# A two-layer streaming encoder on one core: half of layer 0's second shift is read later, three up groups are computed without it, and its output projection is split except for two units

## The chip, the core and the metric

The kernel runs on one core of a Trainium2 chip, one launch for the whole function. The metric is device time in microseconds (us). Arrays are float32.

## What is computed

Two layers over 256 positions of 2048 channels, with one conditioning vector c. What matters of a layer (LN is a layer norm, ALPHA a constant; the four mixers between are not touched by the change):

```
mod = silu(c) @ w_mod[l] + b_mod[l]            # 2048 -> 6 x 2048
shift_m, scale_m, gate_m, shift_f, scale_f, gate_f = mod
h = LN(x) * (1 + scale_m) + shift_m
y = concat(mixers(h @ w_in[l])) @ w_out[l]     # output projection, 2048 x 2048
x = LN(ALPHA * x + (1 + gate_m) * y)
h = LN(x) * (1 + scale_f) + shift_f
gate, val = split(h @ w_up[l])                 # 2048 -> 2 x 5632
y = (silu(causal_conv3(gate) + b_conv) * val) @ w_down[l]
x = LN(ALPHA * x + (1 + gate_f) * y)
```

shift_f is a vector over channels, the same for every position; so its part of `h @ w_up` is one number per column of w_up: `shift_f @ w_up`.

## The kernel before

**Products.** A weight of 1 MB is loaded as `wraw` (two k-tiles of 128 rows by 1024 columns, or four of 512). ScalarE (ACT) casts each half to fp32r as `whi` (L344), VectorE (DVE) writes the rest as `wlo` (L345); activations are split in the same way by `split` (L361: `a`, `hT`). A split product on TensorE (PE) is hi x hi + hi x lo + lo x hi. A plain product takes the fp32 weight `wexact` (0.5 MB a load) and the unsplit activations in one matmul instruction; each of those has two records in the trace. `weights` (L314) makes either kind.

**The output projection.** `out_proj` (L574) makes the 2048 output columns in the chunks 1024, 512 and 512 (`CHUNKS`, L572), each over all 16 k-tiles in units. For layer 0 the second and third chunk, and the first two units of the first (`PLAIN_UNITS`), are plain (`exact`, L703); layer 1 splits all of it. `finish` (L601) applies gate and residual, `norm` (L632) the layer norm, and `to_hN` (L549) turns the result (`ps_xT`, PE) and applies scale and shift into `hN`: four pieces per quarter and half of the positions, on ACT or DVE. k-tile kt of `h` is channels 128 kt to 128 kt + 127.

**The FFN's up projection.** `ffn_up` (L1373) goes through groups of 512 columns: first gate group 0 (`first_group`, L490, plain, straight from `hN`), whose result is turned and copied into `g` (L1405); then value group v0, gate group g1, v1, g2, v2 and so on (`group2`, L417), each four units of four k-tiles, from `hT`, the split of `hN` (L364, L363). Each gate block's convolution and SiLU, `gate_conv` (ACT at L120 and L1418, DVE at L1415), waits in the list `background` and is taken two at a unit; `valued` (L1420) multiplies a value group in.

**The modulation.** Each 128 columns of w_mod are one step of `mods` (L255): a load of 1 MB `wmod`, issued by the SP queue (L192), and one DVE instruction that multiplies by the replicated silu(c) and sums (L193), 192 steps in all. They are a generator, in the fixed order of L255: a layer's shift, scale and gate vectors of 16 steps each. At each unit, `pump` adds the rate of the phase (`RATES`, L35) and takes as many steps as are due; `need` takes those that are missing before a vector is used. A gate vector is turned into a row, written to DRAM (`line`) and read back to all partitions (`gate`) by `gate_rows` (L231). `wmod`, `wraw` and `wlate` tiles share one pool of raw buffers.

The program's order on each engine is the order in which this code calls it, except where a unit's products are held back one step (`pending`, `postponed`).

Of the kernel before, what the change touches and what calls it, by code (L numbers as in the profile page):

```python
# [35 lines left out]
    dict(B=1.3, attend=1.3, C=1.9, out=1.0, out_next=1.55, out_last=0.0, up=0.7, down=0.7, down_next=0.7, down_last=0.0),  # L36
    dict(D=1.0, U=0.0, V=0.0, B=0.0, C=0.0, E=0.9, attend=0.0, out=0.6, out_next=0.6, out_last=0.0, up=0.3, down=0.7, down_next=0.7, down_last=0.0),
# [7 lines left out]
PLAIN_UNITS = 2  # L45

# [40 lines left out]
def encoder_kernel(ctx: ExitStack, tc: tile.TileContext, A: dict, consts: bass.AP, out: bass.AP):  # L87
# [122 lines left out]
    def mod_stream(order):  # L210
        for l, m in order:
            yield from column_steps(l, m)
        while chores:
            yield
            chore()

    def column_steps(l, m):
        sums = keep.tile([P, KT], F32, name=f"sums_{l}_{m}")
        for kt in range(KT):
            last_step[0] = mod_block(l, m, kt, sums[:, kt : kt + 1]).ins.name  # L220
            if kt == KT - 1:
                cols = keep.tile([P, KT], F32, name=f"mod_{l}_{m}")
                dve.tensor_tensor(out=cols, in0=sums, in1=bcol[l][:, m * KT : (m + 1) * KT], op=ALU.add)
                for j in range(KT):
                    MOD[(l, m, j)] = cols[:, j : j + 1]
                if m in (GATE_M, GATE_F):
                    chores.extend(gate_rows(l, m, cols))
            yield
            chore()

    def gate_rows(l, m, cols):  # L231
# [3 lines left out]
        def turn():  # L235
            if pace["phase"] == "up":
# [19 lines left out]
        [(0, GATE_M), (0, SHIFT_F), (0, SCALE_F), (0, GATE_F), (1, SHIFT_M), (1, SCALE_M)]  # L256
# [14 lines left out]
    def need(l, m):  # L271
        rows = m in (GATE_M, GATE_F)
        while (l, m) not in GATE if rows else (l, m, KT - 1) not in MOD:
# [275 lines left out]
    def to_hN(t, q, r, l, m_shift, m_scale, after=None):  # L549
# [10 lines left out]
        for j in range(4):  # L560
            src, dst = ps[:, j * P : (j + 1) * P], hN[q][:, j, t * P : (t + 1) * P]
            sc, sh = MOD[(l, m_scale, 4 * q + j)], MOD[(l, m_shift, 4 * q + j)]
            if t == 0 or j % 2 == 0:
                last_norm[1] = ident_act(dst, src, sc, sh)
                turned[q] = last_norm[1].ins.name
            else:
# [7 lines left out]
    def out_proj(l, stage, w, src, order, gate_of, name, post_g, post_b, before, then, plain=(), bg=0):  # L574
# [112 lines left out]
        for c0, width in CHUNKS:  # L687
# [11 lines left out]
            def load_unit(u, c0, width, nk, units, last):  # L699
# [3 lines left out]
                exact = c0 in plain or (bool(plain) and u < PLAIN_UNITS)  # L703
# [669 lines left out]
    def ffn_up(l, G):  # L1373
# [3 lines left out]
        for c0 in range(0, D_FF, 512):  # L1377
            gi, j0 = c0 // 512, c0 // P

# [10 lines left out]
            def gated(cps, j0=j0):  # L1390
# [3 lines left out]
                for i in range(4):  # L1394
                    background.append(lambda j=j0 + i: gate_conv(j))

            def gated_first(t, ps):
# [8 lines left out]
                if t == 1:  # L1406
                    for i in range(4):
                        background.append(lambda j=i: gate_conv(j))
# [10 lines left out]

            def valued(cps, j0=j0):  # L1420
# [8 lines left out]
            else:  # L1429
                run(group2(w, c0, f"g{l}{gi}", gated))  # L1430
            run(group2(w, D_FF + c0, f"v{l}{gi}", valued, bg=STEPS[l]["up"]))
# [93 lines left out]
    for l in range(DEPTH):  # L1525
# [5 lines left out]
        else:  # L1531
# [14 lines left out]
            plain=(1024, 1536) if l == 0 else (),  # L1546
            bg=STEPS[l]["out"],
        )
        phase(l, "up")
# [47 lines left out]

def _constants():
# [25 lines left out]
def build(inputs):  # L1624
# [7 lines left out]
    direct.update(params=_params(v), gmlp=_gmlp(v), consts=_constants())  # L1632
# [21 lines left out]
```

## Time and profile before

| | |
|---|---|
| median of 3 runs | 2214.95 us (2213.76 to 2219.54) |
| the profiled execution | 2214.94 us |
| its span on the core | 2213.2 us |
| PE busy | 2185.3 us (99%) |
| DVE busy | 1702.1 us (77%) |
| ACT busy | 1075.7 us (49%) |
| POOL (GpSimd) busy | 22.4 us (1%) |
| read from HBM | 604.17 MB, 274 GB/s over the span |

Busy time is a mean over stages. PE is busy nearly always, so the kernel's time is PE's work plus PE's waits; where PE waits, the row of PE's timeline has the wait in square brackets, with what ended it. A matmul's row is longer than the step from one product to the next, since products overlap in the array: a rate is read from the starts of two rows, not from a row's length.

### The profile page before, as it was taken

Reading aid. Unit: us, or ns where it says so; the run is one execution under the profiler, and the core shown is the slowest. Engines: PE = TensorE matmul, PEld = TensorE weight load, DVE = VectorE, ACT = ScalarE, POOL = GpSimd, SP = SyncE. Lnnn points to the kernel's source line nnn. Section 1 sums busy time; section 2 is a strip of 40 time slices with the busy share of each in tenths; the row PEclk is TensorE's granted clock in tenths of the full one; section 3 lists DMA queues with packets and bytes.
Section 4 is the critical chain, followed back from the end, with each engine's and each line's share of the span. In section 5 each row is a group of like instructions: output and inputs, shape, how many; then the busy total and the mean of one; then the engine's idle time right before and its main releaser. Section 6 shows DMA issues by size and latency. Waiting matters only on the chain. (4 is left out here: it accounts for less than half of the span.)

```text
span 2213.2 us, 28318 instructions
## 1 busy us (share of the span) xinstructions
PE 2185.3 (99%) x10852; PEld 1794.0 (81%) x10852; DVE 1702.1 (77%) x2265; ACT 1075.7 (49%) x1652; POOL 22.4 (1%) x38
## 2 busy tenths in 40 slices
PE   9999999999999999999999999999999999999997
PEld 6776875588888888888867988868888888888886
DVE  5657996799898888989958988877765656565776
ACT  3132730655454545545665455465444545464553
POOL 0000000000000000000000000000000000000000
PEclk9999999999999999999999999999999999999999
DMA  9999889598888888888757547856765555555553
GB/s 391 417 376 391 358 332 390 210 350 324 310 333 318 327 313 324 344 332 326 285 215 294 189 157 255 316 210 246 265 211 190 190 190 191 190 210 192 191 195 145
DMA packets 94730, 608.15 MB, mean 275 GB/s; under 512 B 10689, under 2 KB 10881, under 8 KB 29313
## 3 DMA queue, kind: packets, MB, share of 16 engines
q1 hardware_dynamic: 94466, 606.31, 74.0%
q8 instruction: 85, 1.39, 0.2%
q14 instruction: 51, 0.42, 0.0%
q10 hardware_dynamic: 128, 0.03, 0.0%
HBM read 604.17 MB, written 2.13 MB: 274 GB/s over the span
## 5 line engine op out<-in xcount | busy, mean ns | idle before, releaser
L345 DVE TENSOR_TENSOR wlo<-wraw,whi 128x1024 fp32r<-128x1024 f32 (+1 forms) x608 | 729.0, 1214 | 286.3 <-ACT whi L344 273.1
L344 ACT CAST whi<-wraw 128x1024 fp32r<-128x1024 f32 (+1 forms) x608 | 630.9, 1045 | 635.4 <-PE g_c L117 207.8
L193 DVE SCALAR_TENSOR_TENSOR wmod<-wmod,crep 128x2048 f32<-128x2048 f32 x192 | 438.4, 2287 | 72.0 <-DMA wmod<-in_w_mod_dram 71.1
L117 PE MATMUL v_c<-hT,whi 128*128 128x512 f32 x1408 | 489.7, 393 | 0.0
L117 PE MATMUL g_c<-hT,whi 128*128 128x512 f32 x1280 | 445.0, 392 | 0.0
L117 PE MATMUL v_c<-hT,wlo 128*128 128x256 f32 x1408 | 392.5, 279 | 0.0
L117 PE MATMUL d<-whi,a 128*128 128x512 f32 x1344 | 386.5, 389 | 0.0
L117 PE MATMUL g_c<-hT,wlo 128*128 128x256 f32 x1280 | 356.8, 279 | 0.4 <-DVE wlo L345 0.4
L117 PEld LDWEIGHTS v_c<-hT,whi 128*128 128x128 f32 x1408 | 263.6, 187 | 59.2
L117 PEld LDWEIGHTS d<-whi,a 128*128 128x128 f32 x1344 | 252.0, 188 | 52.4
L117 PEld LDWEIGHTS g_c<-hT,whi 128*128 128x128 f32 x1280 | 239.7, 187 | 54.1
L117 PEld LDWEIGHTS v_c<-hT,wlo 128*128 128x128 f32 x1408 | 265.4, 188 | 0.2
L117 PEld LDWEIGHTS g_c<-hT,wlo 128*128 128x128 f32 x1280 | 241.2, 188 | 0.7 <-DVE wlo L345 0.7
L117 PE MATMUL d<-wlo,a 128*128 128x512 f32 x672 | 232.9, 389 | 0.0
L117 PEld LDWEIGHTS d<-wlo,a 128*128 128x128 f32 x672 | 126.1, 188 | 26.2
L363 ACT CAST a<-g 128x512 fp32r<-128x512 f32 x132 | 81.3, 617 | 63.8 <-PE d L117 63.2
L364 DVE TENSOR_TENSOR a<-g,a 128x512 fp32r<-128x512 f32 x132 | 89.0, 686 | 5.1 <-ACT a L363 5.1
L117 PE MATMUL o<-whi,a 128*128 128x512 f32 x320 | 91.6, 393 | 0.0
L501 PE MATMUL first<-wexact,hN 128*128 128x512 f32 x192 | 85.5, 595 | 1.4 <-ACT hN L120 1.0
L1415 DVE SCALAR_TENSOR_TENSOR u<-g,par,u 128x254 f32<-128x254 f32 (+1 forms) x176 | 73.8, 477 | 0.0
L117 PEld LDWEIGHTS o<-whi,a 128*128 128x128 f32 x320 | 60.6, 190 | 12.7
L501 PEld LDWEIGHTS first<-wexact,hN 128*128 128x128 f32 x192 | 35.3, 190 | 41.2 <-issue 34.9
(311 smaller groups left out, 2174.0 us busy)
## 6 DMA issues: line engine op xcount, KB each, us to landing
wmod<-in_w_mod_dram SPq DMA_DIRECT2D x192, 1024.0 KB, 7.2
wraw<-in_ffn_w_up_dram SPq DMA_DIRECT2D x168, 1024.0 KB, 5.1
wraw<-in_ffn_w_down_dram SPq DMA_DIRECT2D x88, 1024.0 KB, 5.0
wexact<-in_w_in_dram SPq DMA_DIRECT2D x64, 512.0 KB, 11.0
wraw<-in_w_in_dram SPq DMA_DIRECT2D x24, 1024.0 KB, 6.1
wraw<-in_w_out_dram SPq DMA_DIRECT2D x22, 1024.0 KB, 6.0
wexact<-in_w_out_dram SPq DMA_DIRECT2D x20, 512.0 KB, 11.6
wexact<-in_ffn_w_up_dram SPq DMA_DIRECT2D x16, 512.0 KB, 5.7
```

The costliest lines, as they stand in the source:

```text
L117: pe.matmul(o, lhsT, rhs, start=start, stop=stop, skip_group_check=True)
L193: i = dve.scalar_tensor_tensor(out=raw, in0=raw, scalar=1.0, in1=crep, op0=ALU.mult, op1=ALU.mult, accum_out=col)
L344: held(act.copy(hi[:, :m], r), "cast")
L345: i = dve.tensor_tensor(out=lo[:, :m], in0=r, in1=hi[:, :m].bitcast(F32), op=ALU.subtract)
L363: act.copy(hi, src)
L364: dve.tensor_tensor(out=lo, in0=src, in1=hi.bitcast(F32), op=ALU.subtract)
L501: i = pe.matmul(ps, hN[kt // 4][:, kt % 4, t * P : (t + 1) * P], parts[kt], start=kt == 0, stop=kt == KT - 1, skip_group_check=True,)
L1415: dve.scalar_tensor_tensor(out=u[:, sh:], in0=x[:, : S - sh], scalar=col(k, j), in1=u[:, sh:], op0=ALU.mult, op1=ALU.add)
```

## The change

- The second and third chunk of layer 0's output projection are made of split products, as in layer 1; the first two units of the first chunk stay plain. With 512 columns a chunk has 8 units.
- The order of the modulation steps is now: gate_m, scale_f, the first 8 k-tiles of shift_f, its last 8 (the late half), 4 steps of gate_f, six new steps (`late_steps`), the rest of gate_f, and so on. `need` asks only for the first 8 k-tiles of layer 0's shift_f. The rate is 0 in chunks two and three, 1.0 in the first gate group and v0 (phase `up_first`), and 0.75 after.
- `to_hN` leaves the shift out for k-tiles 8 to 15 of layer 0's FFN (12 pieces on ACT, 4 on DVE, with one operand less). Gate groups 0 and 1 and value group 0 are computed with that input, three groups of 512 columns.
- In g1, as soon as a unit's products are issued, `renewing` rewrites the hT of that unit's k-tiles, if they are among 8 to 15, with the shift: 8 ACT and 8 DVE instructions of 128x256. v1 and all later groups use it.
- The late half of the vector is made a row (`late_row`: a write to DRAM and a read of 0.5 MB to all partitions, both issued by GpSimd), and `late_steps` load the 1536 columns of w_up for the three groups transposed (six loads of 1 MB, `late`, laid out on the host) and sum them with the row on DVE: 12 instructions of 128x1024, one number per channel.
- That number is added to a gate block ahead of its convolution (`gate_late`, 8 on ACT) and to a value block where it is multiplied in (`value_late`, 4 on DVE and 2 products). Until then v0 and v1 are kept in `value` tiles.

The numbers of instructions go on PE from 10014 to 10142, on DVE from 2051 to 2089, on ACT from 1598 to 1632, on the SP queue from 659 to 657 and on POOL from 43 to 45.

```diff
-    dict(B=1.3, attend=1.3, C=1.9, out=1.0, out_next=1.55, out_last=0.0, up=0.7, down=0.7, down_next=0.7, down_last=0.0),
+    dict(B=1.3, attend=1.3, C=1.9, out=1.0, out_next=0.0, out_last=0.0, up_first=1.0, up=0.75, down=0.7, down_next=0.7, down_last=0.0),
...
+LATE = 8
...
+    def column_steps(l, m, k0=0, k1=KT):
...
+                if (l, m) == (0, SHIFT_F) and k1 == KT:
+                    chores.append(lambda: late_row(cols[:, LATE:KT]))
...
+    def late_row(cols):
+        line = dramp.tile([P, KT - LATE], F32, name="line_late")
+        pool.dma_start(out=line, in_=cols)
+        late["row"] = gatep.tile([P, D], F32, tag="gate", name="late_row")[:, : (KT - LATE) * P]
+        pool.dma_start(out=late["row"], in_=line.rearrange("p k -> (p k)").partition_broadcast(P))
+        return True
+
+    def late_steps():
+        n = (KT - LATE) * P
+        for i in range(6):
+            raw = raw_tile("wlate")
+            nc.sync.dma_start(out=raw, in_=A["late"][i])
+            for h in range(2):
+                part = raw[:, h * n : (h + 1) * n]
+                dve.scalar_tensor_tensor(
+                    out=part, in0=part, scalar=1.0, in1=late["row"], op0=ALU.mult, op1=ALU.mult,
+                    accum_out=late["sums"][:, 2 * i + h : 2 * i + h + 1],
+                )
+            if i % 2 == 1:
+                background.extend(late["then"].pop(0))
+            yield
+            chore()
...
-        [(0, GATE_M), (0, SHIFT_F), (0, SCALE_F), (0, GATE_F), (1, SHIFT_M), (1, SCALE_M)]
+        [(0, GATE_M), (0, SCALE_F), (0, SHIFT_F, 0, LATE), (0, SHIFT_F, LATE, KT)]
+        + [(0, GATE_F, 0, 4), late_steps, (0, GATE_F, 4, KT), (1, SHIFT_M), (1, SCALE_M)]
...
+        last = LATE - 1 if (l, m) == (0, SHIFT_F) else KT - 1
...
+            without = (l, m_shift) == (0, SHIFT_F) and 4 * q + j >= LATE
...
-                exact = c0 in plain or (bool(plain) and u < PLAIN_UNITS)
+                exact = u < plain and c0 == 0
...
+                if l == 0 and j0 < 8:
+                    late["then"].append([lambda j=j0 + i: gate_late(j) for i in range(4)])
...
+            def gate_late(j):
+                x = G[j // 4][:, j % 4, :]
+                ident_act(x, x, 1.0, late["sums"][:, j : j + 1])
+                gate_conv(j)
...
+            def value_late(i):
+                v0, v1 = late["values"]
+                for j in (2 * i, 2 * i + 1):
+                    g = G[0][:, j, :]
+                    dve.scalar_tensor_tensor(
+                        out=g, in0=v0[:, j, :], scalar=late["sums"][:, 8 + j : 9 + j], in1=g, op0=ALU.add, op1=ALU.mult
+                    )
+                g = G[1][:, 2 * i : 2 * i + 2, :]
+                dve.tensor_tensor(out=g, in0=g, in1=v1[:, 2 * i : 2 * i + 2, :], op=ALU.mult)
...
+    def renewing(g):
+        units, load, products, end, bg = g
+        def then(item, u):
+            products(item, u)
+            for kt in range(max(LATE, 4 * u), 4 * u + 4):
+                h, col = hN[kt // 4][:, kt % 4, :], MOD[(0, SHIFT_F, kt)]
+                hi, lo = (x[:, kt % 2, :] for x in hT[kt // 2][:2])
+                ident_act(hi, h, 1.0, col)
+                dve.scalar_tensor_tensor(
+                    out=lo, in0=h, scalar=col, in1=hi.bitcast(F32), op0=ALU.add, op1=ALU.subtract
+                )
+        return units, load, then, end, bg
...
-            plain=(1024, 1536) if l == 0 else (),
+            plain=PLAIN_UNITS if l == 0 else 0,
```

**VectorE where v0 starts.** The last splits of `hT`, the modulation steps, the two copies of gate group 0's result and the first weights of v0 (`wlo`), before:

```order
L364 TENSOR_TENSOR hT_2332<-hN3_2169,hT_2332 128x2x256
L193 SCALAR_TENSOR_TENSOR wmod_2368,sums_0_5_2367<-wmod_2368,crep_104 128x2048
L364 TENSOR_TENSOR hT_2333<-hN3_2169,hT_2333 128x2x256
L193 SCALAR_TENSOR_TENSOR wmod_2371,sums_0_5_2367<-wmod_2371,crep_104 128x2048
L345 TENSOR_TENSOR wlo_2377<-wraw_2374,whi_2376 128x1024
L345 TENSOR_TENSOR wlo_2381<-wraw_2374,whi_2380 128x1024
L193 SCALAR_TENSOR_TENSOR wmod_2384,sums_0_5_2367<-wmod_2384,crep_104 128x2048
L1405 COPY g_2350<-ps_gT_2353 128x4x128
L1405 COPY g_2350<-ps_gT_2361 128x4x128
```

and with the change:

```order
L402 TENSOR_TENSOR hT_2494<-hN3_2331,hT_2494 128x2x256
L402 TENSOR_TENSOR hT_2495<-hN3_2331,hT_2495 128x2x256
L195 SCALAR_TENSOR_TENSOR wmod_2529,sums_0_3_1599<-wmod_2529,crep_104 128x2048
L195 SCALAR_TENSOR_TENSOR wmod_2532,sums_0_3_1599<-wmod_2532,crep_104 128x2048
L195 SCALAR_TENSOR_TENSOR wmod_2535,sums_0_3_1599<-wmod_2535,crep_104 128x2048
L195 SCALAR_TENSOR_TENSOR wmod_2538,sums_0_3_1599<-wmod_2538,crep_104 128x2048
L1461 COPY g_2512<-ps_gT_2515 128x4x128
L1461 COPY g_2512<-ps_gT_2523 128x4x128
L383 TENSOR_TENSOR wlo_2544<-wraw_2541,whi_2543 128x1024
```

Four steps in a row and the copies now stand ahead of v0's first `wlo`; before, two steps did, and both `wlo` came ahead of the copies.

**ScalarE in g1.** The casts of g1's third unit (`whi_2807`, `whi_2811`), the rewriting of k-tiles 8 to 11 (`hT_2492`, `hT_2493`) and the casts of the fourth unit, with the change:

```order
L382 CAST whi_2807<-wraw_2805 128x1024
L382 CAST whi_2811<-wraw_2805 128x1024
L122 ACTIVATE hT_2492<-hN2_2330,mod_0_3_1600 128x256 x2
L122 ACTIVATE hT_2493<-hN2_2330,mod_0_3_1600 128x256
L382 CAST whi_2853<-wraw_2851 128x1024
L382 CAST whi_2857<-wraw_2851 128x1024
L122 ACTIVATE hT_2493<-hN2_2330,mod_0_3_1600 128x256
```

Three of the four new instructions stand ahead of the fourth unit's casts; before, nothing stood between the casts of two units there.

**VectorE in g2.** The end of the late sums, the work with them, and the weights of g2's last unit (`wlo_3314`), with the change:

```order
L383 TENSOR_TENSOR wlo_3262<-wraw_3259,whi_3261 128x1024
L383 TENSOR_TENSOR wlo_3266<-wraw_3259,whi_3265 128x1024
L258 SCALAR_TENSOR_TENSOR wlate_3301,late_118<-wlate_3301,late_row_2693 128x1024 x2
L1479 SCALAR_TENSOR_TENSOR g_2512<-value_2742,late_118,g_2512 128x256 x2
L1483 TENSOR_TENSOR g_2951<-g_2951,value_3170 128x512
L1479 SCALAR_TENSOR_TENSOR g_2512<-value_2742,late_118,g_2512 128x256 x2
L1483 TENSOR_TENSOR g_2951<-g_2951,value_3170 128x512
L383 TENSOR_TENSOR wlo_3314<-wraw_3311,whi_3313 128x1024
```

All the rows between the two units' `wlo` are new at this place.

## Rows read from the trace of the kernel before

**Rows 1.** The page: span, and busy time of each engine with its instructions.

```profile
span 2213.2 us, 28318 instructions
PE 2185.3 (99%) x10852; PEld 1794.0 (81%) x10852; DVE 1702.1 (77%) x2265; ACT 1075.7 (49%) x1652; POOL 22.4 (1%) x38
```

**Rows 2.** The chain that ended last: start us, us, what. Layer 1, split groups.

```profile
1518.14 22.19 PE g_c L117 x128
...
1961.98 239.42 PE d L117 x1056
```

**Rows 3.** Stretch of chunks two and three: us, busy of PE, PEld, DVE, ACT, POOL; PEclk, DMA.

```profile
346.16:401.10 54.94, 54.94 (x130) 24.27 (x129) 33.87 (x57) 7.34 (x18) 1.55 (x2) 1.00 0.95 382
```

**Rows 4.** VectorE's timeline: start us, us, line, operation; layer 0, ahead of chunk two.

```profile
341.45 2.28 DVE L193 SCALAR_TENSOR_TENSOR wmod<-wmod,crep 128x2048 f32<-128x2048 f32 x1
...
343.87 1.29 DVE L604 TENSOR_TENSOR yg<-o,gate 128x512 f32<-128x512 f32 x2
```

**Rows 5.** TensorE's timeline where the projection ends: layer 0, then layer 1.

```profile
401.10 1.04 PE L557 MATMUL ps_xT<-cst,xn 128*128 128x128 f32 x8
402.24 3.70 PE L501 MATMUL first<-wexact,hN 128*128 128x512 f32 x8
...
1462.26 0.39 PE L117 MATMUL o<-whi,a 128*128 128x512 f32 x1
...
1464.09 0.70 PE L501 MATMUL first<-wexact,hN 128*128 128x512 f32 x1
```

**Rows 6.** VectorE's timeline where v0 starts.

```profile
425.00 0.68 DVE L364 TENSOR_TENSOR hT<-hN,hT 128x512 fp32r<-128x512 f32 x1
425.60 2.28 DVE L193 SCALAR_TENSOR_TENSOR wmod<-wmod,crep 128x2048 f32<-128x2048 f32 x1
...
432.89 2.28 DVE L193 SCALAR_TENSOR_TENSOR wmod<-wmod,crep 128x2048 f32<-128x2048 f32 x1
...
435.10 1.28 DVE L1405 COPY g<-ps_gT 128x512 f32<-128x512 f32 x2
436.31 1.22 DVE L345 TENSOR_TENSOR wlo<-wraw,whi 128x1024 fp32r<-128x1024 f32 x1
437.44 1.66 DVE L1415 SCALAR_TENSOR_TENSOR u<-g,par,u 128x255 f32<-128x255 f32 x4
```

**Rows 7.** TensorE's timeline: the first lo product of v0, and the first product of g1.

```profile
434.07 0.36 PE L117 MATMUL v_c<-hT,wlo 128*128 128x256 f32 x1
...
456.13 0.39 PE L117 MATMUL g_c<-hT,whi 128*128 128x512 f32 x1
```

**Rows 8.** ScalarE's timeline in v0: two casts, four first steps of the convolution.

```profile
433.50 2.00 ACT L344 CAST whi<-wraw 128x1024 fp32r<-128x1024 f32 x2
...
436.42 2.08 ACT L120 ACTIVATE u<-g,par 128x256 f32<-128x256 f32 x4 [0.92 <-DVE g L1405]
```

**Rows 9.** DMA issues: KB each, median us from issue to landing.

```profile
wraw<-in_ffn_w_up_dram SPq DMA_DIRECT2D x168, 1024.0 KB, 5.1
...
gate<-line SPq DMA_DIRECT2D x4, 1024.0 KB, 5.7
...
cst<-in_consts_dram SPq DMA_DIRECT2D x1, 448.0 KB, 14.6
```

**Rows 10.** TensorE's timeline, waits in the output projection's first chunk.

```profile
294.67 14.00 PE L117 MATMUL o<-wexact,ya 128*128 128x512 f32 x32 [1.02 <-DMA wexact<-in_w_out_dram]
...
311.94 1.22 PE L117 MATMUL o<-wlo,a 128*128 128x512 f32 x2 [1.00 <-DVE wlo L345]
...
315.28 1.09 PE L117 MATMUL o<-whi,a 128*128 128x512 f32 x4
```

**Rows 11.** A stretch right behind one of those waits; columns as in rows 3.

```profile
313.00:315.00 2.00, 2.00 (x6) 1.61 (x5) 2.00 (x2) 1.98 (x3) 0.00 (x0) 0.50 1.03 430
```

**Rows 12.** GpSimd's timeline: one small operation, twice, in the third chunk.

```profile
391.37 0.99 POOL L147 TENSOR_TENSOR rs_o0p<-rs_o0p,mhalf 128x1 f32<-128x1 f32 x1 [75.22 <-DVE rs_o0p L536]
398.07 0.56 POOL L147 TENSOR_TENSOR rs_o0r<-rs_o0r,mhalf 128x1 f32<-128x1 f32 x1 [5.71 <-DVE rs_o0r L680]
```

More of the change, by code (lines that the diff above doesn't have):

```diff
@@ L210, in mod_stream @@
     def mod_stream(order):
-        for l, m in order:
-            yield from column_steps(l, m)
+        for entry in order:
+            yield from entry() if callable(entry) else column_steps(*entry)
         while chores:
@@ L215, in mod_stream @@
             chore()
-    def column_steps(l, m):
-        sums = keep.tile([P, KT], F32, name=f"sums_{l}_{m}")
-        for kt in range(KT):
-            last_step[0] = mod_block(l, m, kt, sums[:, kt : kt + 1]).ins.name
[L221 to L224, printed above, removed]
+    columns = {}
+    def column_steps(l, m, k0=0, k1=KT):
+        if k0 == 0:
+            columns[(l, m)] = [keep.tile([P, KT], F32, name=f"{n}_{l}_{m}") for n in ("sums", "mod")]
+        sums, cols = columns[(l, m)]
+        for kt in range(k0, k1):
+            last_step[0] = mod_block(l, m, kt, sums[:, kt : kt + 1]).ins.name
+            if kt == k1 - 1:
+                dve.tensor_tensor(
+                    out=cols[:, k0:k1], in0=sums[:, k0:k1], in1=bcol[l][:, m * KT + k0 : m * KT + k1], op=ALU.add
+                )
+                for j in range(k0, k1):
@@ L225, in column_steps @@
                     MOD[(l, m, j)] = cols[:, j : j + 1]
-                if m in (GATE_M, GATE_F):
+                if m in (GATE_M, GATE_F) and k1 == KT:
                     chores.extend(gate_rows(l, m, cols))
+                if (l, m) == (0, SHIFT_F) and k1 == KT:
+                    chores.append(lambda: late_row(cols[:, LATE:KT]))
+            yield
+            chore()
+    late = {"sums": keep.tile([P, 12], F32, name="late"), "then": []}
+    def late_row(cols):
[4 more added lines that the diff above has]
+        return True
@@ L572, in encoder_kernel, with out_proj @@
     CHUNKS = ((0, 1024), (1024, 512), (1536, 512))
-    def out_proj(l, stage, w, src, order, gate_of, name, post_g, post_b, before, then, plain=(), bg=0):
+    def out_proj(l, stage, w, src, order, gate_of, name, post_g, post_b, before, then, plain=0, bg=0):
         nkt = len(order)
@@ L1418, in gate_conv, with valued_late @@
                 act.activation(out=x, in_=u, func=AF.Silu)
+            def value_late(i):
[7 more added lines that the diff above has]
+                dve.tensor_tensor(out=g, in0=g, in1=v1[:, 2 * i : 2 * i + 2, :], op=ALU.mult)
+            def valued_late(cps):
+                v = actp.tile([P, 1024], F32, tag="act", name="value").rearrange("p (j s) -> p j s", j=4)
+                late.setdefault("values", []).append(v)
+                for i, t in enumerate(second(cps)):
+                    dve.tensor_tensor(out=v[:, i, :], in0=cps[i][:, :S], in1=t, op=ALU.add)
+                if len(late["values"]) == 2:
+                    late["then"].append([lambda i=i: value_late(i) for i in range(2)])
             def valued(cps, j0=j0):
```

41 lines of the change are left out of this document (28 added, 13 removed).

## The prediction

> **What bounds the kernel now.** I read the page first, for which engine is full; then the chain of waits, for what PE's products cost when nothing stops them; then PE's timeline where the change is made; then DVE's and ACT's, since they feed PE. The page says PE: busy for 2185.3 of 2213.2 us [rows 1]. In the chain, a group of 128 pairs in layer 1 takes 22.19 us without a gap, so a unit of four k-tiles takes 5.55 us and a pair .347; and 1056 split products of 512 columns take 239.42 us, .2267 us each [rows 2]. So the time is PE's work plus PE's waits. An edit counts if it takes products away, or if it makes DVE or ACT late by more than their lead over PE. The profiled execution took 2214.94 us, the median is 2214.95: the sum may be made against either. A measurement of this kernel tells 0.3%, 6.6 us, from no change; so faster is below 2208.3 and slower above 2221.6.
>
> **The products.** Chunks two and three of layer 0's projection last 54.94 us, all but two of the 130 records there are those of the 64 plain products, at a granted clock of 1.00 [rows 3]: .858 us a product. Each becomes three split ones: 192 x .2267 = 43.5 us [rows 2]. PE saves 54.94 - 43.5 = **11.4 us**.
>
> By what the page has for one plain product, .858 against three of .2267, four would cost .907, so a plain product is a little cheaper than four split ones [rows 2, 3]. The Trainium skill, "FP8 and Floating Point Precision", section "TensorE Precision Notes", says that true FP32 makes four passes through the array; by that the saving would be a quarter of 54.94, 13.7 us, and the time 2.3 us less than I give. The rows have both durations, so I go by them.
>
> What hides the feeding: in 43.5 us DVE has 16 more splits of 1.13 us [rows 6], 18.1, but 7 modulation steps of 2.21 fewer there, 15.5. It was busy for 33.87 of 54.94 us [rows 3], so it comes to some 36.5 of 43.5. ACT gets 16 casts of 1.00 [rows 8] on top of 7.34. Both keep up; were that cover gone, each late split would cost 1.13 us. The two modulation vectors that layer 1 uses are still ready, as six inserted steps don't shift the order enough to be waited for.
>
> **Five new waits of PE.** None of them is in the trace of before; each is worked out from the nearest rows. "Late" means against a PE that goes on without a gap.
>
> - (a) *Start of chunk two.* Its first unit was plain and needed no work of DVE but the load. Now a split has to be made behind a modulation step and two gate products: these end at 343.87 + 2 x .60 = 345.07, one x instruction of the same kind comes between (.60), and the split takes 1.13: 346.8 [rows 4, 6]. PE is through chunk one at 346.16 [rows 3] and has about .2 us of hi products. Late by **.4** (0 to 1).
> - (b) *End of chunk three.* The other half's products cover the layer norm; split, they are shorter. Layer 0 had 1.14 us from the end of the projection to the next group's first product; layer 1, which is in that form already, has 1464.09 - (1462.26 + .23) = 1.60 [rows 5]. **+.5**.
> - (c) *Start of v0.* DVE's order, quoted above, is now: last two splits of hT, four modulation steps, two copies, then the first weights of v0. From 425.00 on: 2 x .60, 4 x 2.21, 2 x .60, 1.13 = 12.4, and (b) on top: 437.9 [rows 6]. Before, the first lo product came at 434.07 and v0 ended at 456.13 [rows 7]. PE has four hi products (.91) to do and waits, so v0 ends at 437.9 + 22.19 - .91 = 459.2, 3.1 late, of which .5 is (b): **2.6**. The load for this unit needs the buffer of the first of the four steps, free at 428.9, and lands 5.1 us later [rows 9], at 434.0; cast and split follow at 435.0 and later, so the load doesn't decide. If the steps were already running in the waits ahead of the hT splits it could be nothing, and if the load lands later it is 1 us more: 0 to 3.6.
> - (d) *Rewriting hT in g1.* An hT half may be overwritten when PE has read it for the last time. Three such rewrites stand on ACT ahead of the casts of g1's fourth unit, and the third waits until .69 us before the end of PE's third unit (two of its pairs are left). A rewrite takes .52 us (the four u instructions' 2.08) and a cast 1.00 [rows 8]: the hi weights are there .85 after PE wants them. Its four hi products take .91, and the lo weights come 1.13 after the cast: .2 more. **1.1** (0 if the rewrites of DVE and ACT slip behind the casts' place, 2 if DVE's three wait as well).
> - (e) *DVE in v1 and g2.* From the first late step to the weights of g2's fourth unit DVE has: 12 half steps (half of a 2.21 step and its reading of the sum, 1.14 as I take it), 13.7; 16 u instructions of .41, 6.6; 13 splits of 1.13, 14.7; 4 additions of about .40, 1.6; the value blocks, 4 x .41 and 2 x .60, 2.8 [rows 6]. That is 39.4, and it starts 2 us behind v1's first product, 41.4. PE wants these weights 7 units and four products on, 39.7 [rows 2]. **1.7** (0 to 3: at 1.22 a half step it would be 2.7). After it, DVE has 18 to 20 us of work per 22.19 and catches up; ACT's 8 `gate_late` of .52 have room.
>
> The sum: -11.4 + .4 + .5 + 2.6 + 1.1 + 1.7 = **-5.1**, so 2214.94 - 5.1 = **2209.8 us**. The other edits cost nothing: `to_hN` drops an operand, and the six loads of 1 MB stand on SP's queue in the place of modulation loads of the same size that move behind them; with eight loads of weights for 16 half as large, the queue has two instructions fewer.
>
> **Rivals.**
>
> A. *The waits are hidden.* DVE and ACT start some of this work earlier than I let them, since I took the order as rigid and their waits as those of before. For it: DVE was busy for only 77% [rows 1], and 0 is an end of (a), (c), (d) and (e). Against: in v0 the order on the engine leaves no choice. With only (b) the time is 2214.94 - 10.9 = 2204.0, with not even that 2203.5; with half of the rest hidden, 2206.9.
>
> B. *PE's clock falls behind each wait.* One wait of 1.00 us in the first chunk was followed by a stretch at a granted clock of .50, the lower of the two levels (1.2 of 2.4 GHz) [rows 10, 11]: from 311.94 to 315.28 PE made 8 products in 3.34 us instead of 1.81, a loss of 1.5. Another wait of 1.02 us was followed by 32 records in 14.00 us, .44 each, as in the full-speed stretch [rows 3, 10]. So one of two. Four of my waits, (a), (c), (d) and (e), could each cost 1.5: up to +6.0, 2215.8; one or two of them give 2211.3 to 2212.8.
>
> C. *The late row comes too late: slower.* The row is written and read back by GpSimd's queue. Its eight sums are ready ahead of v0's last unit, at about 450, and DVE wants the row 2 us behind g1's end, at 459.2 + 22.2 + 1.1 + 2 = 484.5: 34 us for two DMAs in a row. If they take longer, the first late step blocks the head of DVE's queue, with v1's and g2's splits behind it, and PE stops. The nearest rows have 5.7 us for a row of 1 MB read to all partitions, so 11.4 for two; the farthest is 14.6 [rows 9], and a small POOL operation took .99 us under a busy DVE against .56 beside an idle one [rows 12], a factor of 1.77: 2 x 14.6 x 1.77 = 51.7, 17.7 late, 2227.5. It decides from 34 us on, and makes the kernel slower than before by over 0.3% from 34 + 11.8 = 46 us on. No row shows a DMA issued by GpSimd. The Trainium skill, "SBUF — State Buffer", section "SBUF: two separate sides", says that such a DMA's descriptors are written by GpSimd, which some DVE instructions lock out of a port they share; it advises another queue. The rows bear it out only so far as that factor of 1.77 goes, and DVE does have gaps between such instructions.
>
> D. *The change doesn't do what it says.* If the loads limited the split chunks, PE would not get faster. But the weights are the same 8 MB (eight loads of 1 MB for 16 of half that), seven loads of steps leave, and the stretch moved 382 GB/s [rows 3], 21 MB in all where now some 14 are needed; I give it nothing of its own.
>
> **How the numbers follow.** The forecast, waits within their bounds and the clock mostly up: .45. A: .25, B: .22, C: .08. The predicted time is the forecast's, 2209.8. Faster (below 2208.3): all of A and a little over a third of the forecast, .25 + .17 = .42. Slower (above 2221.6): most of C, .07. The same: .51. The range goes from A's end, 2203.5, to B's end with (e) at its upper price, 2215.8 + 1.0 = 2216.8, and leaves out C and some tails.
>
> **What would show it.** In the changed profile, chunks two and three should be two rows of 192 products in about 43.5 us. PE's timeline should have waits in brackets of about .4 (ended by wlo at chunk two), 2.6 to 3.1 (wlo, v0's first unit), 1 (whi and wlo, g1's fourth unit) and 1.7 (wlo, g2's fourth unit). The first late step should start as soon as g1's additions are done: an idle stretch there, ended by a DMA into the row, is C. The prediction is wrong if v0's wait is not there, if the chunks take much more than 43.5, if the granted clock is .50 behind the waits (B), or if waits come in places that I didn't name.

## The result: 8 us slower, and the profile after

The changed kernel takes **2222.2 us** (median of 8 runs, 2220.51 to 2229.78) against 2214.12 for the kernel before: 1.0037 of it, 95% interval 1.0028 to 1.0047. Forecast were 2209.8 us and a range that ended at 2216.8. The profiled execution is the slowest of the eight, 2229.78 us.

The page after, span and busy time, against [rows 1]:

```profile
span 2228.0 us, 28480 instructions
PE 2193.1 (98%) x10916; PEld 1808.3 (81%) x10916; DVE 1736.1 (78%) x2315; ACT 1095.5 (49%) x1686; POOL 22.1 (1%) x40
```

Chunks two and three of layer 0's projection, against [rows 3] (same columns):

```profile
347.44:391.05 43.61, 43.38 (x191) 35.59 (x191) 35.56 (x57) 19.74 (x32) 1.55 (x2) 1.00 0.83 313
```

They take 43.6 us instead of 54.9; forecast was 43.5. (The stretch begins behind two products of chunk two and ends with .39 us in which PE waits ahead of `ps_xT`. Counted from chunk two's first product, at 346.58, the 192 products take 44.1 us, of which .40 is a wait: 43.7.) DVE was busy for 35.56 us of it (forecast 36.5). PE's waits from there to layer 1 (waited for: us in total, times, longest); before, this view of the same stretch has one wait, of .4 us for `wlo` in a late group:

```profile
PE d L119 <- ACT whi L382: 3.3, 2, 1.7
PE v_c L119 <- DVE wlo L383: 1.6, 1, 1.6
PE g_c L119 <- DVE wlo L383: 0.9, 1, 0.9
PE g_c L119 <- ACT whi L382: 0.8, 1, 0.8
PE v_c L119 <- ACT whi L382: 0.3, 1, 0.3
PE o L119 <- DVE wlo L383: 0.2, 1, 0.2
PE ps_gT L1460 <- ACT gt L1457: 0.2, 1, 0.2
PE ps_xT L595 <- ACT xn L122: 0.2, 1, 0.2
```

`o` is (a), `ps_xT` is (b), the two of `v_c` and `ps_gT` are (c), `g_c` for `whi` is (d) and `g_c` for `wlo` is (e). All five waits are there, at the places named. The first row, at the start of the down projection, was not in the forecast. The chain that ended last shows the second thing that was not, in layer 1, whose code the change does not touch [rows 2]:

```profile
1524.52 22.61 PE g_c L119 x128
```

A group has 128 pairs, each one product of 512 columns with hi weights and one of 256 with lo weights. Without a wait a group took 22.19 us before and takes 22.61 here, .42 more, at a granted clock of 1.00. PE's timeline in a group of layer 1, first before and then after, shows where:

```profile
1599.44 0.39 PE L117 MATMUL v_c<-hT,whi 128*128 128x512 f32 x1
1599.67 0.28 PE L117 MATMUL v_c<-hT,wlo 128*128 128x256 f32 x1
1599.79 0.39 PE L117 MATMUL v_c<-hT,whi 128*128 128x512 f32 x1
1600.02 0.28 PE L117 MATMUL v_c<-hT,wlo 128*128 128x256 f32 x1
1600.13 0.39 PE L117 MATMUL v_c<-hT,whi 128*128 128x512 f32 x1
```

```profile
1599.96 0.40 PE L119 MATMUL v_c<-hT,whi 128*128 128x512 f32 x1
1600.20 0.28 PE L119 MATMUL v_c<-hT,wlo 128*128 128x256 f32 x1
1600.31 0.40 PE L119 MATMUL v_c<-hT,whi 128*128 128x512 f32 x1
1600.56 0.28 PE L119 MATMUL v_c<-hT,wlo 128*128 128x256 f32 x1
1600.67 0.40 PE L119 MATMUL v_c<-hT,whi 128*128 128x512 f32 x1
1600.91 0.28 PE L119 MATMUL v_c<-hT,wlo 128*128 128x256 f32 x1
1601.02 0.40 PE L119 MATMUL v_c<-hT,whi 128*128 128x512 f32 x1
```

Before, a pair takes .35 us (.23 and .11) and each is like the last. After, three pairs make a figure of .35, .36 and .35 that repeats, 1.06 us where three would take 1.04. The rows show no wait for an engine: PE has fallen into another rhythm.

How the 14.8 us between the two spans add up, by the first product of each stage: -3.5 up to v2 (522.69 to 519.19), +5.2 in the rest of layer 0's up groups, +4.6 in the down projection, -.3 to layer 1's up groups, +8.9 in these, -.1 to the end. Of the -3.5, +.4 stood already at chunk two's first product.

### The profile page after: what moved, and what is told of

Read it like the earlier page. It is cut to its first block, busy times and chain, and to the rows that moved or that the text cites. A ratio compares the mean times of both kernels' runs of the same rounds, so it can differ in the third digit from the quotient of the medians.

```text
span 2228.0 us, 28480 instructions
## 1 busy us (share of the span) xinstructions
PE 2193.1 (98%) x10916; PEld 1808.3 (81%) x10916; DVE 1736.1 (78%) x2315; ACT 1095.5 (49%) x1686; POOL 22.1 (1%) x40
## 5 line engine op out<-in xcount | busy, mean ns | idle before, releaser
L383 DVE TENSOR_TENSOR wlo<-wraw,whi 128x1024 fp32r<-128x1024 f32 (+1 forms) x620 | 739.5, 1212 | 285.8 <-ACT whi L382 271.6
L119 PE MATMUL v_c<-hT,whi 128*128 128x512 f32 x1408 | 496.1, 398 | 0.3 <-ACT whi L382 0.3
L119 PE MATMUL g_c<-hT,whi 128*128 128x512 f32 x1280 | 451.3, 398 | 0.8 <-ACT whi L382 0.8
L119 PE MATMUL o<-whi,a 128*128 128x512 f32 x416 | 120.4, 390 | 0.0
L119 PEld LDWEIGHTS o<-whi,a 128*128 128x128 f32 x416 | 77.9, 188 | 16.5 <-ACT whi L382 0.4
L119 PE MATMUL o<-wlo,a 128*128 128x512 f32 x208 | 72.5, 392 | 1.2 <-DVE wlo L383 1.1
```

What stands on the lines that cost most here:

```text
L119: pe.matmul(o, lhsT, rhs, start=start, stop=stop, skip_group_check=True)
L383: i = dve.tensor_tensor(out=lo[:, :m], in0=r, in1=hi[:, :m].bitcast(F32), op=ALU.subtract)
```

## The experiments

All kernels with their times (number of runs, ratio to the kernel before with its interval), and the us that most groups without a wait take in layers 0 and 1 in the profile taken of each. Each kernel is compared with times of the kernel before that were taken with it. Those scatter too: where a_apart, b_apart, a_up70 and b_split were timed, the kernel before had a median of 2214.50, but ten of its 35 times lay between 2218 and 2230, so these four ratios are nearer to 1 than the medians are. No profile was taken of such an execution.

| kernel | us | ratio | layer 0 | layer 1 |
|---|---|---|---|---|
| the change | 2222.2 (8) | 1.0037 [1.0028, 1.0047] | 22.61 | 22.61 |
| after_again | 2222.35 (1) | | 22.61 | 22.19 |
| a_late_small | 2221.3 (10) | 1.0027 [1.0015, 1.0039] | 22.61 | 22.19 |
| b_pad_all | 2222.47 (5) | 1.0035 [1.0022, 1.0048] | 22.61 | 22.19 |
| b_pad_act | 2243.64 (4) | 1.0130 [1.0108, 1.0152] | 22.61 | 22.33 |
| b_pad_w | 2236.75 (4) | 1.0098 [1.0081, 1.0115] | 22.61 | 22.61 |
| b_split | 2220.1 (10) | 1.0021 [1.0005, 1.0037] | 22.19 | 22.19 |
| a_apart | 2218.4 (12) | 1.0008 [0.9992, 1.0023] | 22.29 | 22.29 |
| b_apart | 2218.6 (10) | 1.0008 [0.9995, 1.0021] | 22.29 | 22.29 |
| a_up70 | 2224.02 (10) | 1.0035 [1.0020, 1.0050] | 22.61 | 22.19 |
| b_pad_reset | 2229.05 (4) | 1.0067 [1.0053, 1.0080] | 22.55 | 22.55 |
| a_reset | 2228.35 (4) | 1.0064 [1.0050, 1.0077] | 22.55 | 22.55 |
| a_reset_74 | 2224.94 (5) | 1.0049 [1.0035, 1.0062] | 22.55 | 22.55 |
| a_apart_fix | **2211.93** (12) | 0.9986 [0.9978, 0.9995] | 22.29 | 22.29 |
| a_fix | 2221.53 (10) | 1.0028 [1.0011, 1.0045] | 22.61 | 22.61 |
| a_fix_small | 2216.63 (10) | 1.0001 [0.9990, 1.0013] | 22.61 | 22.19 |

### Is it where the tiles lie?

The change adds one lasting tile, the late sums, of 64 bytes a partition. It lies ahead of the pools of weights, activations and slots, which all start 64 bytes further than before, no longer at multiples of 128. That was the first theory for the rhythm.

```diff
-    late = {"sums": keep.tile([P, 12], F32, name="late"), "then": []}
+    late = {"sums": smallp.tile([P, 12], F32, tag="late", name="late", bufs=1), "then": []}
```

> The changed kernel, with the 64-byte tile of the late sums moved from the pool of lasting tiles, which lies ahead of all others in SBUF, to the pool of small tiles, which lies behind weights and activations. The order on every engine is unchanged; only the address of the weight, activation and slot tiles moves back by 64 bytes, to multiples of 128, as in the kernel before. Theory (the slower pace of the up groups comes from where the tiles lie): groups without a wait take 22.19 us in both layers instead of 22.61, and the time falls by some 11 to 18 us from 2222, to about 2207 to 2212. Rival (the new order of work or the waits put PE into a slower rhythm): groups stay at 22.61 and the time at 2222.

```diff
+    keep.tile([P, 16], F32, name="pad")
     rms_eps = keep.tile([P, 2], F32, name="rms_eps")
```

> The kernel before, with an unused tile of 64 bytes in the pool of lasting tiles, so that weights, activations and slots all lie 64 bytes further. The order on every engine is unchanged. Theory (addresses): groups of both layers take 22.61 us instead of 22.19, 44 x .42 = 18 us in all if every group is slow, so up to 2232. Rival (order or waits): 22.19 and 2214.

```diff
+    padp = ctx.enter_context(tc.tile_pool(name="padp", bufs=1))
     actp = ctx.enter_context(tc.tile_pool(name="actp", bufs=10))
...
+    padp.tile([P, 16], F32, name="pad")
```

> The kernel before, with the unused 64 bytes between the pools of weights and of activations: only activations (hT, a) and slots move. If PE's moving operand hT is what counts: 22.61 us a group and up to 2232. If the stationary weights count: 22.19 and 2214. Rival (order or waits): 22.19 and 2214.

In b_pad_w the lines of `actp` and `padp` stand ahead of that of `splitp`.

> The kernel before, with the pool of activations put ahead of that of the weights and the unused 64 bytes between them: weights (whi, wlo) and slots lie 64 bytes off a multiple of 128, the activations on one. If the stationary weights count: 22.61 us a group and up to 2232. If the moving operand hT counts: 22.19 and 2214. Rival (order or waits): 22.19 and 2214.

The theory is half right; a_late_small came out as its rival had it in layer 0 and as the theory had it in layer 1. **b_pad_all** computes what the kernel before computes, in the same order on every engine, with 64 bytes that nobody uses, and is 8 us slower: as slow as the change. Its PE timeline, first products of two groups in a row, in layer 0 and in layer 1:

```profile
479.32 0.40 PE L117 MATMUL v_c<-hT,whi 128*128 128x512 f32 x1
...
501.93 0.40 PE L117 MATMUL g_c<-hT,whi 128*128 128x512 f32 x1
...
1547.72 0.40 PE L117 MATMUL v_c<-hT,whi 128*128 128x512 f32 x1
...
1569.91 0.40 PE L117 MATMUL g_c<-hT,whi 128*128 128x512 f32 x1
```

22.61 in layer 0, 22.19 in layer 1, at the same addresses of hT. Moving activations and slots by 64 bytes, with the weights in place, costs 29 us, the down projection in it (246.6 us in layer 0 instead of 240.1). b_pad_w, with the two pools exchanged, the activations at multiples of 128 and weights and slots 64 bytes off, costs 22 us (its down projection 242.3). So neither the weights' nor the activations' place is alone the one that counts, and a place that costs nothing in one layer costs 9 us in the other. And **a_late_small**, with the weights and activations where they were before, keeps the slow rhythm in layer 0. Addresses move the rhythm; they alone don't set it.

### Does one program have both rhythms?

> The changed kernel, unchanged: a second profile of the same program. Theory (the up groups can run in a fast or a slow rhythm, and what came before chooses): its eight times lie at 2220.5 to 2224 and once at 2229.8, and the profile of the slowest has 22.61 us a group in both layers; a run at about 2222 then has 22.19 us a group in layer 1 with the same addresses and order. Rival (addresses alone choose): 22.61 in both layers again, whatever the time.

The same program, 2222.35 us, first products of two groups in layer 0, then in layer 1:

```profile
565.55 0.40 PE L119 MATMUL v_c<-hT,whi 128*128 128x512 f32 x1
...
588.17 0.40 PE L119 MATMUL g_c<-hT,whi 128*128 128x512 f32 x1
...
1569.83 0.40 PE L119 MATMUL g_c<-hT,whi 128*128 128x512 f32 x1
...
1592.01 0.40 PE L119 MATMUL v_c<-hT,whi 128*128 128x512 f32 x1
```

22.62 and 22.18: layer 1 runs in the quick rhythm here and in the slow one in the execution of 2229.78 us, with the same addresses and the same order. The 7.4 us between the two executions are that: 21 groups of .42 make 8.8, and the second execution was 1.6 later at the start of the down projection. The ten times of a_fix, below, fall into two heaps for the same reason as it seems: five from 2215.2 to 2218.7, five from 2224.3 to 2229.5; its one profile, of 2225.07 us, has both layers slow. Of the faster heap there is no profile.

### Taking the turn of hi and lo away

`group2` has a flag for the order all hi, then all lo. Set for the up groups:

```diff
-            run(group2(w, D_FF + c0, f"v{l}{gi}", valued, bg=STEPS[l]["up"]))
+            run(group2(w, D_FF + c0, f"v{l}{gi}", valued, bg=STEPS[l]["up"], apart=True))
```

and so for the gate groups and in the changed kernel.

> The changed kernel, with the products of each up unit in another order: all products with hi weights first, then all with lo weights, as in the input projection's groups, instead of hi and lo in turn. Same products, same tiles. Theory (the order in turn can fall into a slower rhythm of three pairs in 1.06 us, and SBUF addresses and what came before choose it): a unit of 16 products of .227 and 16 of .120 takes 5.55 us in every group, so groups without a wait take 22.2 in both layers; the waits for lo weights (1.56 in v0, .89 in g2) shrink or go, since these are wanted 3.6 us after the unit's start instead of .9; time about 2208 to 2213. Rival (the addresses slow PE's reads in any order): groups stay at 22.6 and only the waits go: about 2219.

> The kernel before with the same other order of the up products. Theory (rhythm): its groups run in the fast rhythm already, 22.19, so 22.2 and a time within 3 us of 2214. Rival (the order of products is worth something by itself): below 2208.

The groups of both kernels without a wait now take 22.29 us, with few exceptions, at both places of the tiles, that of the kernel before and that of the change; the chain of b_apart has in layer 1:

```profile
1519.04 22.29 PE g_c L117 x128
```

So at these two places the slow rhythm belongs to the turn of 512- and 256-column products. The places of b_pad_act and b_pad_w were not tried in this order, and there the down projection, which has products of 512 columns only, was slower too. The order hi-then-lo costs .10 a group against the quick rhythm, which is what b_apart pays for: two layers with 21 such groups make 42 x .10 = 4.2 us, measured 4.1 by the medians and 3.0 by the spans of the two profiles, in which the kernel before loses 1.5 in its own last groups. Both forecasts missed: b_apart is 1.6 us above its range, a_apart 5.4 above its own. The waits for lo weights in a_apart's up groups went, but 3.3 us of waits for hi came in v0 and g1; it starts the down projection 4.6 us ahead of b_apart and loses that there, with the unforeseen wait (245.13 us against 240.07).

A weaker form, hi-then-lo in the first unit of a group only, was meant to break the rhythm:

```diff
-            if apart:
+            if apart or (turn and u == 0):
```

> The kernel before with the unused 64 bytes of b_pad_all, and in the first unit of each up group the hi products first and then the lo ones, by halves; the other three units in turn as before. Theory (the slow rhythm is kept up by the turn of hi and lo and can be broken): layer 0's groups fall from 22.61 to 22.2 to 22.35 us, and the time from 2222.5 to about 2214 to 2217. Rival (addresses alone): three units in four stay slow, 22.5 and 2220.

> The changed kernel with the same first units. Theory (rhythm): 22.2 to 22.35 a group in both layers, and v0's and g2's waits for lo weights (1.56 and .89) go; the two waits at the start of the down projection stay (4.6): about 2211 to 2215. Rival (addresses alone): 22.5 a group, 2219 to 2221.

Both theories missed. In most groups of both kernels the three units in turn fall into the slow figure soon behind the first unit's last lo product: 22.55, in layer 1 too. What comes before does choose, but this was a choice for the worse.

### The wait at the start of the down projection

ScalarE there, after (columns as in [rows 8]):

```profile
908.82 0.62 ACT L401 CAST a<-g 128x512 fp32r<-128x512 f32 x1 [2.63 <-PE d L119]
914.26 0.62 ACT L401 CAST a<-g 128x512 fp32r<-128x512 f32 x1 [4.82 <-PE d L119]
914.79 3.89 ACT L382 CAST whi<-wraw 128x1024 fp32r<-128x1024 f32 x4
```

PE there:

```profile
915.88 1.20 PE L119 MATMUL d<-whi,a 128*128 128x512 f32 x4 [1.65 <-ACT whi L382]
```

An `a` may be cast only when PE has released a pair of activations. The second of two such casts stands ahead of the weights of two units and waits 4.82 us; PE, at 915.88, has then waited 1.65 for the weights. The same happens once more at 989. In the kernel before, one `a` stands there between the two casts of one unit and those of the next:

```profile
903.13 0.61 ACT L363 CAST a<-g 128x512 fp32r<-128x512 f32 x1
905.77 1.05 ACT L344 CAST whi<-wraw 128x1024 fp32r<-128x1024 f32 x1 [2.03 <-PE d L117]
907.13 1.05 ACT L344 CAST whi<-wraw 128x1024 fp32r<-128x1024 f32 x1 [0.30 <-PE d L117]
908.09 0.61 ACT L363 CAST a<-g 128x512 fp32r<-128x512 f32 x1
```

The order of the casts changes with the units at which the modulation steps fall, so their rate was set back:

```diff
-    dict(B=1.3, attend=1.3, C=1.9, out=1.0, out_next=0.0, out_last=0.0, up_first=1.0, up=0.75, down=0.7, down_next=0.7, down_last=0.0),
+    dict(B=1.3, attend=1.3, C=1.9, out=1.0, out_next=0.0, out_last=0.0, up_first=1.0, up=0.7, down=0.7, down_next=0.7, down_last=0.0),
```

> The changed kernel with the rate of the modulation steps in the later up groups at 0.7, as before, instead of 0.75; the first groups' rate stays. It changes the order in which ScalarE casts the gated activations and the down projection's weights where that projection starts: weights no longer behind two activations in a row. Theory (the two waits of 1.65 us at the start of the down projection are the price of that order): the down projection takes 240.1 instead of 244.7 us; time 4 to 5 us less for the same rhythm of the up groups. Rival (the waits come from buffers that the new steps hold): 244.7 again.

The two waits are gone, the casts stand as in the kernel before, and the down projection takes 240.08 us: the theory's part holds. The time does not fall, because the slower rate leaves one modulation step too many: PE's timeline at the end of layer 1's output projection has

```profile
1470.02 1.97 PE L595 MATMUL ps_xT<-cst,xn 128*128 128x128 f32 x8 [6.60 <-ACT xn L122]
```

where the last step of layer 1's second scale now stands in the layer norm on DVE. Behind this wait the granted clock was .50 from 1470 to 1474 us. The rate of .75 had a reason.

**a_reset_74** tried another pair of rates with the first units of a_reset:

```diff
-    dict(B=1.3, attend=1.3, C=1.9, out=1.0, out_next=0.0, out_last=0.0, up_first=1.0, up=0.75, down=0.7, down_next=0.7, down_last=0.0),
+    dict(B=1.3, attend=1.3, C=1.9, out=1.0, out_next=0.0, out_last=0.0, up_first=0.85, up=0.74, down=0.7, down_next=0.7, down_last=0.0),
```

> As a_reset, with the rates of the modulation steps at .85 (first groups) and .74, chosen so that ScalarE has at most one weight pair behind two activations where the down projection starts, and as many steps done by layer 1's output projection as in the change. Theory: the waits of 4.6 us at the down projection's start go, nothing else changes: about 2206 to 2211, faster than both kernels. Rival (those waits come from elsewhere, or the later steps make layer 1 wait as in a_up70): as a_reset or slower.

One of the two waits went (242.8 us), 2.3 us of a wait at layer 1's norm came, and the rhythm stayed at 22.55 in most groups: a miss.

### The split without the moved steps

```diff
-                exact = c0 in plain or (bool(plain) and u < PLAIN_UNITS)
+                exact = bool(plain) and c0 == 0 and u < PLAIN_UNITS
```

> The kernel before with chunks two and three split and nothing else: the seven modulation steps stay beside them and the shift stays whole. Theory (DVE is the cover): it has 33.87 + 16 x 1.13 = 52 us of work for 43.5 us of products, so PE waits some 8 us for lo weights and the 11.4 us are mostly given back: 2208 to 2214 if the up groups keep their rhythm. Rival (the steps can wait, the weights go first): chunks of 43.5 us and 2203.

PE's waits (columns as above):

```profile
PE o L117 <- DVE wlo L345: 4.5, 3, 3.5
PE o L117 <- ACT thi L344: 2.3, 1, 2.3
PE o L117 <- DVE tlo L345: 2.0, 1, 2.0
PE ps_xT L557 <- ACT xn L120: 1.7, 2, 1.4
```

10.5 us, and behind the longest of them the granted clock fell (.59 from 358 to 362 us, .50 from 380 to 384, there between a wait of 2.3 and one of 2.0). The first group starts at 407.87 instead of 402.24: the 11.4 us and 5.6 more are given back (.9 of that stood already at chunk two's first product). The up groups keep 22.19. Both forecasts missed: 2220.1 is 6 us above the theory's range. So beside the seven steps the split does not pay; with these steps moved out, for which the shift had to come late, the chunks take 43.6 us.

### Both causes taken out

To the edit of a_up70 comes one of layer 1's rates, here on the change (a_fix), on a_late_small (a_fix_small) and on a_apart (a_apart_fix):

```diff
-    dict(D=1.0, U=0.0, V=0.0, B=0.0, C=0.0, E=0.9, attend=0.0, out=0.6, out_next=0.6, out_last=0.0, up_first=0.3, up=0.3, down=0.7, down_next=0.7, down_last=0.0),
+    dict(D=1.0, U=0.0, V=0.0, B=0.0, C=0.0, E=0.9, attend=0.0, out=0.8, out_next=0.8, out_last=0.0, up_first=0.3, up=0.3, down=0.7, down_next=0.7, down_last=0.0),
```

> a_apart with the rate of the later up groups at 0.7 and, so that layer 1's second scale is still in time, the rate in layer 1's output projection at 0.8 instead of 0.6. Theory (the change is worth what the sum of products and waits says, and the rest is rhythm and ScalarE's order at the down projection): the down projection takes 240.1 us instead of 245.1, layer 1's output projection 87.5; some 5 us below b_apart's 2218.6 and a_apart's 2218.4, about 2213.5. Rival (something else of the change costs 5 us more): 2218.

> The changed kernel with the same two rates and its own order of products. The down projection takes 240.1 us, so about 4.6 us below the change's 2222 in the same rhythm (layer 0 slow, layer 1 fast): 2217.5; with both layers fast 2208.5, with both slow 2227.

> a_fix with the tile of the late sums in the pool of small tiles, so that weights and activations lie at the addresses of the kernel before. The same three times by rhythm: 2208.5, 2217.5 or 2227; if addresses alone chose the rhythm, 2208.5.

The stage of the down projection in the change and in a_fix (columns as in [rows 3]):

```profile
903.06:1147.80 244.74, 241.03 (x1061) 197.83 (x1058) 209.44 (x242) 124.67 (x165) 1.48 (x2) 1.00 0.84 314
```

```profile
902.02:1142.10 240.08, 239.79 (x1061) 198.14 (x1058) 207.03 (x241) 125.17 (x165) 1.48 (x2) 1.00 0.85 313
```

The 4.66 us between them are the price of the order of the casts. **a_apart_fix takes 2211.93 us**, 6.7 less than b_apart by the medians, 4.9 by the spans of the two profiles (2216.2 and 2211.3). Against the kernel before it is .9986, .9978 to .9995, or 2.3 us by the medians: a gain of .1%, less than the .3% that the prediction took for telling. Stage by stage its gain over b_apart was larger: the first product of v2, in b_apart and in a_apart_fix, is

```profile
523.00 0.40 PE L117 MATMUL v_c<-hT,whi 128*128 128x512 f32 x1
...
515.77 0.40 PE L119 MATMUL v_c<-hT,whi 128*128 128x512 f32 x1
```

7.2 us earlier, and the down projection starts 7.5 earlier. 2.6 of that go again by layer 1's first split up group, most of it in the output projection's norm: a wait of 1.6 for `xn`, where the rates still put a step too late, and a granted clock of .52 behind it, from 1460 to 1462. So the change is worth about what the sum had said, -5.1, where both kernels share one rhythm; but that the totals are so near is luck. In this order the waits for lo of v0 and g2 are gone (1.56 and .89 in the change), waits for hi of 1.0 and 1.1 stand in v0 and g1, and the loss in layer 1 comes from the rates and is in no term of the sum. The profiles of a_fix and a_fix_small have layer 0 in the slow rhythm; a_fix_small's two lowest times, 2209.4 and 2209.8, are where the forecast was and 1 us above the 2208.5 of two quick layers, but there is no profile of them.

## Why the prediction was wrong

**The products: right.** 43.7 us for the 192 products against 43.5; the saving is 11.3. By the four passes of the Trainium skill ("FP8 and Floating Point Precision", section "TensorE Precision Notes") the saving would have been 13.7, which the rows do not bear out.

**The five waits: right in place and kind, four of five in size.** A bracket counts from the end of the row ahead, which is later than the step to the next product would be; what a wait costs is read from the starts. (a) .24 in the bracket; lo comes .63 behind the hi product instead of .23, so .40 for .4 (two hi products stand ahead of it, .45 us and not .2, and the lo weights were as much later). (b) .23 for `xn`, so that the gap is 1.59 as in layer 1: +.45 for .5. (c) From the first group's last stretch to v0's end 37.17 us against 34.47: +2.7 for 2.6; the waits are .24, .29 and 1.56. (d) .83 for `whi` in the bracket; with the first steps behind it and the lo weights, 1.3 by the starts, for 1.1. (e) .89, by the starts 1.04, for 1.7: DVE was ahead of my account by some .7 us. From chunk two's first product to v2 the sum is -3.9 in one profile and -3.5 in the other; -5.1 was forecast. The difference is the slow rhythm in the groups between, with .6 in v1, where no loss was forecast, and the restarts behind the waits (the first two products behind one are .33 apart instead of .23). Counted from the start of the span, v2 is 3.5 and 2.4 earlier, since these two executions reach chunk two .4 and 1.1 later than the one of before.

**The rivals.** A did not come: none of the five waits is hidden. B did not come: the granted clock is 1.00 behind each of these waits, of .8 to 1.6 us. C did not come: the two DMAs of the late row took 5.7 and 7.5 us, 13 in all of the 34 it had, and DVE went into the first late step without a wait:

```profile
late_row<-line_late POOLq DMA_DIRECT2D x1, 512.0 KB, 7.5
...
line_late<-mod POOLq DMA_DIRECT2D x1, 4.0 KB, 5.7
```

```profile
474.89 1.21 DVE L258 SCALAR_TENSOR_TENSOR wlate<-wlate,late_row 128x1024 f32<-128x1024 f32 x1
```

These are the rows that the prediction lacked. The stall of GpSimd's DMAs that the Trainium skill warns of ("SBUF — State Buffer", section "SBUF: two separate sides") is not to be seen in them. Beside these two DMAs DVE ran only tensor_tensor and scalar_tensor_tensor; what its other instructions would do, no run here shows. D did not come: the chunks run at the speed of their products and moved 313 GB/s.

**The step that failed** is the one that the prediction hardly wrote down: "The other edits cost nothing", and the use of .347 us a pair, read from one row of layer 1 [rows 2], as a property of the instruction. It is a property of a rhythm. The groups took .42 more: 17 of layer 0 behind g2, 7.1 us, of which 5.2 show, since the kernel before lost 1.5 in its own last groups and the change has a few quick units there; and in some executions 21 of layer 1, 8.9 us. The price was in the trace of before. Its one wait inside an up group is in g10, the last gate group of layer 0; its last value group, v10, follows without a wait:

```profile
861.92 0.39 PE L117 MATMUL g_c<-hT,wlo 128*128 128x256 f32 x1 [0.42 <-DVE wlo L345]
...
878.74 0.40 PE L117 MATMUL v_c<-hT,whi 128*128 128x512 f32 x1
...
901.38 0.71 PE L117 MATMUL d<-whi,a 128*128 128x512 f32 x2
```

From 878.74 to 901.38 are 22.64 us, and the pairs take .35, .35 and .36 in turn from the wait on. The forecast put waits of this kind into v0, g1 and g2, with 17 groups behind the last of them, at no price but their own length. With .42 for each of these groups, less the 1.5 that the kernel before lost itself, the sum would have been some 5.6 us higher, by an estimate from these rows: 2215.4, and the range wider upward. None of the four rivals has such a term.

**The second that failed** is also in "The other edits cost nothing", and in "After it, DVE has 18 to 20 us of work per 22.19 and catches up; ACT's 8 `gate_late` of .52 have room". That is about busy time, not about order. I compared the orders at the places where the change puts new work and not at the start of the down projection, 380 us later, where a rate of .75 instead of .7 had put two casts of activations ahead of the weights: 4.6 us.

-3.5 + 5.2 + 4.6 is 6.3, and with layer 1 in the quick rhythm the second profile ends at +7.3: the median's +8 is accounted for within 1 us.

**What stays open** is why PE falls into the one rhythm or the other. Shown is that without the turn of hi and lo products it is gone at the two places tried, that 64 bytes of address change it, that the order of products just before changes it, and that one program has both. A wait inside a group is a candidate that no run tests by itself. With weights and activations at the addresses of the kernel before (that kernel, b_split, a_late_small, a_fix_small), the profiles show a lasting slow stretch only behind such a wait, in layer 0, and groups of 22.19 (one of 22.26) where none came before in the layer; with 64 bytes more, b_pad_all is slow in layer 0 without any wait. What happens on PE in the .02 us that a figure loses was not seen: the rows show starts, and no engine that is waited for.

## What to carry to other kernels

A pace that is read from a row is a measurement of a state; where the whole time rests on one pace, ask what would happen at 2% more, and compare an edit with a control that holds it (here the order hi-then-lo, at 22.29 in the three kernels that have it). Look in the trace of before for the places where the pace already slips, however late they come. Before a result of less than 1% is put down to an edit, add a few unused bytes to the kernel before: here that alone made 8 and 29 us. And when a rate or a table moves work, read the order of the engines at the next stage's start too: two casts in a row that wait for the consumer, at two places, cost 4.7 us where 11.4 were gained.

## What was not expected of the hardware

- Alternating products of 512 and 256 columns run at 22.19, 22.33 or 22.61 us for 128 pairs, at a granted clock of 1.00 and without a wait, and at 22.55 where the first unit has hi and then lo; all hi and then all lo at 22.29 in a_apart, b_apart and a_apart_fix.
- An unused tile of 64 bytes between weights and activations costs 29 us (b_pad_act, 1.0130); there the down projection's products of 512 columns slow down too, 246.6 us in layer 0 for 1056 instead of 240.1.
- The length of a wait did not say whether the clock falls: in the change the granted clock was 1.00 behind two waits of 1.65 us, in a_apart_fix .52 behind one of 1.56, in the kernel before .50 behind one of 1.00 [rows 10, 11], and in b_split .59 behind one of 3.5 and .50 in a stretch behind one of 2.3 that has another of 2.0.
- A DMA of 4 KB that GpSimd issued landed after 5.7 us, one of 512 KB after 7.5, beside a busy DVE.
